# A two-layer streaming trunk in split fp32: the first input block's rows carry the first norm's scales, the second norm's mean squares are summed on all partitions, and the last store is issued by ScalarE's queue

## The chip, the cores and the metric

The kernel runs on one core of one Trainium2 chip. Its time is the device time of one execution in microseconds, given as the median of the runs beside the lowest and highest of them.

## The reference

The input x is 512 frames of 1024 features. One layer (DEPTH is 1) is computed: a first RMSNorm, a wide projection into three branches (A: six heads of forgetting attention, "fox"; B: four heads of a gated linear recurrence in chunks, "hgrn"; C: a causal depthwise convolution of 31 taps over 256 channels), three sigmoid gates that merge the branches, an output projection with a residual, and then a second RMSNorm with a gated feed-forward network and another residual.

```python
def rmsnorm(x, g):
    y = x32 * lax.rsqrt(jnp.mean(x32 * x32, axis=-1, keepdims=True) + EPS)
    return y * g
...
h = rmsnorm(x, norm_mix_g[l])
z = h @ w_in[l]
(fq, fk, fv, ff, hq, hf, hi, hg, ca, cb, gl) = jnp.split(z, IN_SPLITS, axis=-1)
...                                   # ya: attention, yb: recurrence, yc: convolution
gates = jax.nn.sigmoid(gl + gate_b[l])
merged = gates[:, :, 0] * (ya @ wb_a) + gates[:, :, 1] * (yb @ wb_b) + gates[:, :, 2] * (yc @ wb_c)
x = x + merged @ w_out[l]
h2 = rmsnorm(x, norm_ffn_g[l])
gate_in, value_in = jnp.split(h2 @ w_up[l], 2, axis=-1)
x = x + (jax.nn.silu(causal_dwconv(gate_in, ...)) * value_in) @ w_down[l]
```

## The kernel before

Activations are held transposed: features on the 128 partitions, the 512 frames along the row, in eight blocks (`x0` to `x7`). Every fp32 factor is split into a high and a low part (`x0h`, `x0l`; weights `wh_...`, `wl_...`), and each product is three matmuls: high by high, high by low, low by high. A block of 128 output columns over 1024 features is thus a unit of 24 matmuls of 128x512 into one PSUM bank. A weight unit is loaded by one DMA of SyncE's queue (`wr_...`), cast by ScalarE (`wh_...`) and subtracted by VectorE (`wl_...`). The norms are applied late: the products are made from x times the norm's gain, and the result is multiplied by the frame's reciprocal root mean square (`n1rB`, `n2rB`, the same row on all partitions) when VectorE takes it out of PSUM (`evac`).

No engine's order is written by hand. Every operation is recorded in a `Plan` by `record` (so that the profile gives nearly all of them line 110, and tiles tell them apart); `schedule` then plays the program through with a cost for each operation. Each of the five engines takes, of the operations whose inputs are there, the one of the lowest priority number for which a buffer is free, and the order that comes out is what the engines run, each strictly in it. The priority is the place in the program, less a large number for classes such as `FIRST` (loads and splits of the input), `EVAC` (evacuations) and `YOUT`. The counts of buffers are in `CAPS`: 75 full rows of 128x512 (kind "s"), eight PSUM banks (kind "ps") of which at most five hold projections ("mm") and at most six hold everything else ("aux"). An operation that starts a tile is passed over as long as its kinds are used up, and one of a higher number goes ahead.

In the stretch that the prediction speaks of, the third and last unit of the branch-B output gate (`hg`) is followed by the first merge gates: `gate(n)` makes three units `gl` (one for each branch), each evacuated into a row `gr`. Six `gate` calls stand ahead of the first `merge`. Between these units the last pieces of hgrn heads 2 and 3 and the six fox heads are woven in. A head of the recurrence is a chain of small steps: `khT` (transposes of the decayed keys), `pl` (scores within a block, at seven levels), `pst` (state), `pi` (output). VectorE and ScalarE make each step's operands (`d`, `ed`, `ql`, `kl`) and take its result (`at`, `st`, `ob`). A fox head's scores `sp` lie in "aux" banks until VectorE adds the bias and takes the minimum in one instruction (`dd`, with its accumulator row `mn`). The convolution is 60 tap instructions of VectorE (`cv`, two tiles of 30) that run when VectorE has nothing of lower number; their inputs are the rows `xca`.

The first norm's gains are the first eight columns of `pr`, which a DMA of its own brings in. The second norm sums eight squares in `acc2`; `norm_rstd` multiplies its four blocks by a column of ones on TensorE (`n2ms`, frames on the partitions), takes the root there in four columns, and `spread` transposes them (`n2rT`), writes them to memory (`n2dr`) and reads them back on all partitions (`n2rB`).

Of the kernel before, what the change touches and what calls it, by code (L numbers as in the profile page):

```python
# [10 lines left out]
F32 = mybir.dt.float32  # L11
F32R = mybir.dt.float32r
# [7 lines left out]
KT = D // P  # L20
# [27 lines left out]
for _name, _w in (("ident", 128), ("ones", 128), ("onesD", 32)):  # L48
# [1 line left out]
    _n += _w  # L50
NCST = _n
CAPS = {"s": 75, "bm": 2, "tiny": 24, "wraw": 3, "whi": 3, "wlo": 3, "ps": 8, "mm": 5, "aux": 6,
        "d": 2, "ed": 3, "cB": 4, "dd": 3, "pp": 3, "pT": 8}
NCB = NM * (NM + 1) // 2 * P
NLV = 2
NAHEAD = 6
NWARM = 5
FIRST, WPREP, STAT, EVAC, YOUT = -4000000, -3000000, -2000000, -1000000, -1000000


# [4 lines left out]
class Plan:  # L65
# [73 lines left out]
    def schedule(self):  # L139
        ops = self.ops  # L140
        last = {}
        for op in ops:
            op.left = len(op.deps)
            op.ready = 0.0
            for d in op.deps:
                d.users.append(op)
            for n in op.uses:
                last[n] = last.get(n, 0) + 1
        used = {k: 0 for k in self.caps}
        live = set()  # L150
        free = {e: 0.0 for e in ("tensor", "vector", "scalar", "gpsimd", "sync")}
        soon = {e: [] for e in free}
        now_ = {e: [] for e in free}
        releases = []
        for op in ops:
            if not op.left:
                heapq.heappush(soon[op.eng], (op.ready, op.seq, op))
        t, done, order = 0.0, 0, []
        while done < len(ops):
            while releases and releases[0][0] <= t:  # L160
                _, n = heapq.heappop(releases)
                for k in self.kind[n]:
                    used[k] -= 1
            for e in free:
                while soon[e] and soon[e][0][0] <= t:
                    op = heapq.heappop(soon[e])[2]
                    heapq.heappush(now_[e], (op.pri, op.seq, op))
            moved = False
            for e in free:
                if free[e] > t or not now_[e]:  # L170
                    continue
                put = []
                while now_[e]:
                    it = heapq.heappop(now_[e])
                    op = it[2]
                    need = {}
                    for n in op.uses:
                        if n not in live:
                            for k in self.kind[n]:
                                need[k] = need.get(k, 0) + 1  # L180
                    if all(used[k] + c <= self.caps[k] for k, c in need.items()):
                        for n in op.uses:
                            live.add(n)
                            last[n] -= 1
                        for k, c in need.items():
                            used[k] += c
                        op.start = t
                        op.end = t + op.dur
                        free[e] = op.end
                        for n in op.uses:  # L190
                            if not last[n]:
                                heapq.heappush(releases, (op.end + op.lat, n))
                        for u in op.users:
                            hop = 0.0 if (u.eng == e == "tensor") else op.lat
                            u.ready = max(u.ready, op.end + hop)
                            u.left -= 1
                            if not u.left:
                                heapq.heappush(soon[u.eng], (u.ready, u.seq, u))
                        order.append(op)
                        done += 1  # L200
                        moved = True
                        break
                    put.append(it)
                for it in put:
                    heapq.heappush(now_[e], it)
            if moved:
                continue
            nxt = [f for e, f in free.items() if f > t and now_[e]]
            nxt += [s[0][0] for s in soon.values() if s and s[0][0] > t]
            nxt += [max(s[0][0], free[e]) for e, s in soon.items() if s]  # L210
            if releases:
                nxt.append(releases[0][0])
            nxt = [x for x in nxt if x > t]
            if not nxt:
                raise RuntimeError("no instruction can start: " + str(
                    {e: [(o[2].seq, o[2].uses) for o in now_[e][:3]] for e in now_}) + str(used))
            t = min(nxt)
        self.length = max(op.end for op in ops)
        return order
# [57 lines left out]


@with_exitstack
def body(ctx: ExitStack, tc, xT, wct, wt3, wt1, wdn, par, cst, rst, msk, cmk, out):  # L280
    cpool = ctx.enter_context(tc.tile_pool(name="cpool", bufs=1))
    spool = ctx.enter_context(tc.tile_pool(name="spool", bufs=CAPS["s"]))
    wpool = ctx.enter_context(tc.tile_pool(name="wpool", bufs=3))
# [12 lines left out]
    def slot(name, dt=F32, kind=None):  # L296
        return nc.tile(spool, [P, S], dt, "s", nm(name), ("s", kind) if kind else ("s",))
# [78 lines left out]
        nc.vector.scalar_tensor_tensor(lo, src, g, hi.bitcast(F32), op0=ALU.mult, op1=ALU.subtract)  # L376
        return hi, lo

    def evac(ps, name, rb):
        with nc.at(EVAC):  # L380
            t = slot(name)
            nc.vector.tensor_tensor(t, ps, rb, op=ALU.mult)
        return t

    def strided(t, offset, dims):
        return bass.AP(t.tensor, t.offset + offset, [list(t.ap[0]), *map(list, dims)])

    def rsqrt(v, n, name):
        t = tiny(name + "t", n, I32)
        nc.vector.tensor_single_scalar(t, v.bitcast(I32), 1, op=ALU.logical_shift_right)  # L390
        y = tiny(name + "y", n)
        nc.vector.tensor_scalar(y.bitcast(I32), t, -1, 0x5f3759df, op0=ALU.mult, op1=ALU.add)
        for it in range(3):
            a = tiny(name + "a", n)
            nc.vector.scalar_tensor_tensor(a, y, -0.5, y, op0=ALU.mult, op1=ALU.mult)
            nc.vector.tensor_tensor(a, a, v, op=ALU.mult)
            y2 = tiny(name + f"y{it}", n)
            nc.vector.scalar_tensor_tensor(y2, a, 1.5, y, op0=ALU.add, op1=ALU.mult)
            y = y2
        return y  # L400
# [46 lines left out]
    with nc.at(FIRST):  # L447
        nc.table("sigmoid_and_others")
        for _ in range(NWARM):
            nc.tensor.matmul(wps[:, :256], warm[:, :P], warm[:, :256], start=True, stop=True)  # L450
    cuts = ((0, 1), (1, 2), (2, 3), (3, 4), (4, 6), (6, 8))
    xg, w0, sums = [], [], []
    xs = [slot(f"x{kt}") for kt in range(KT)]

    def first_weights():
        k0, k1 = cuts[len(w0)]
        src = wt3[k0 // 2][:, (k0 % 2) * 384:(k0 % 2) * 384 + (k1 - k0) * 384]
        raw = nc.tile(bpool, [P, 2 * S], F32, "bm", nm("wr_hi"), ("bm",)) if len(w0) in (3, 4) else None
        w0.append(wunit(src, (k1 - k0) * 384, f"hi{len(w0)}", FIRST, raw))

    for kt in range(KT):
        with nc.at(FIRST):
            nc.sync.dma_start(xs[kt], xT[:, kt, :])
            if kt == 0:
                nc.sync.dma_start(pr[:, :KT], par[:, :KT])
            if kt == 4:
                nc.sync.dma_start(pr[:, KT:], par[:, KT:])
        if kt in (0, 1, 2, 3, 5):
            first_weights()
        with nc.at(FIRST):  # L470
            xg.append(split_scaled(xs[kt], pc("g1", kt), f"x{kt}"))
        with nc.at(STAT):
            q = slot(f"n1sq{kt}")
            added = nc.scalar.activation(q, xs[kt], AF.Square)
            if kt:
                nc.vector.tensor_tensor(sums[0], sums[0], q, op=ALU.add)
            else:
                sums.append(q)
# [448 lines left out]
    merged, gates, x1, xg2 = [], [], [], []  # L927

    def gate(n):
        gates.append([evac(gemm_c(15 + 3 * n + br, xg, f"gl{n}{br}"), f"gr{n}{br}", rb1) for br in range(3)])  # L930

    def merge(n):
        gts = gates[n]
# [26 lines left out]


    acc2 = None
    for n in range(KT):
        ps = gemm_c(47 + n, merged, f"wo{n}")
        with nc.at(EVAC):
# [6 lines left out]
            else:  # L972
                acc2 = q
    with nc.at(EVAC):
        rt2, rb2 = norm_rstd([acc2], "n2")


    gT = []
# [14 lines left out]
    for n in range(KT):  # L993
# [6 lines left out]
        for c0, c1 in parts:  # L1000
            with nc.at(EVAC):
                nc.vector.tensor_tensor(x1[n][:, c0:c1], ps[:, c0:c1], x1[n][:, c0:c1], op=ALU.add)
            nc.sync.dma_start(out[n][:, c0:c1], x1[n][:, c0:c1])

    nc.issue(tc)

# [1 line left out]
def _layout(i):  # L1008
# [49 lines left out]
    for L in LEVELS:  # L1058
# [4 lines left out]
    c = np.ascontiguousarray  # L1063
    return {
        "xT": c(x.T.reshape(KT, P, S).transpose(1, 0, 2)), "wct": c(wct), "wt3": c(wt3), "wt1": c(wt1),
        "wdn": c(wdn), "par": c(par), "cst": c(cst), "rst": c(rst), "msk": c(msk), "cmk": c(cmk)}


_ORDER = ("xT", "wct", "wt3", "wt1", "wdn", "par", "cst", "rst", "msk", "cmk")


# [14 lines left out]
```

## Time and profile before

| quantity | value |
|---|---|
| median of 3 runs | 804.49 us (804.33 to 804.51) |
| the profiled execution's own time | 804.38 us |
| its span, first to last instruction | 802.5 us |
| TensorE busy | 797.6 us, 99% of the span |
| VectorE, ScalarE, GpSimd busy | 496.4, 336.6, 86.0 us |

The span is what the trace covers; the own time holds 1.9 us more around it. Busy times are of the whole span, so an engine that is half busy in the mean can be nearly full in one stretch. The "chain that ended last" is followed back from the last instruction to whatever released it at each step, and the time that it spends on an engine is the time that a change must shorten to be seen.

### The profile page before, as it was taken

The page shows a single profiled execution, that of the slowest core. Times are in us where ns is not written, and L with a number is a line of the kernel's source. Part 1 is how long each engine was busy: PE and PEld are TensorE (multiplying, and loading weights), DVE is VectorE, ACT ScalarE, POOL GpSimd, SP SyncE. Part 2 cuts the span into 40 slices and gives each one's busy share as a digit, 9 for nine tenths or more (in the row PEclk, how much of TensorE's full clock was granted, in tenths as well). Part 3 has the DMA queues.
Part 4 walks back from the last instruction along what each step waited for, and adds up shares of the span by engine and source line. Part 5 has one row for each costly group of instructions (what it writes and reads, how often), then busy time and mean ns, then how long its engine had stood idle before and what let it go on. Part 6 is the DMA issues. An engine that isn't in the chain of part 4 may idle for free.

```text
span 802.5 us, 10175 instructions
## 1 busy us (share of the span) xinstructions
PE 797.6 (99%) x3911; PEld 677.0 (84%) x3911; DVE 496.4 (62%) x804; ACT 336.6 (42%) x547; POOL 86.0 (11%) x78
## 2 busy tenths in 40 slices
PE   9999999999999999999999999999999999999998
PEld 8889999888888888888888888888888888888886
DVE  6588898988888878556655465555555455222221
ACT  7247556554656328433244254333333333111110
POOL 2000000100122000114422021111101111000000
PEclk9999999999999999999999999999999999999999
DMA  8522132422477222323422322322322332334320
GB/s 306 182 69 83 60 118 79 106 100 79 120 166 181 93 104 80 118 103 133 145 97 87 119 84 100 105 94 91 105 100 85 105 99 82 102 112 128 101 86 26
DMA packets 30880, 86.96 MB, mean 108 GB/s; under 512 B 3640, under 2 KB 7786, under 8 KB 30832
## 3 DMA queue, kind: packets, MB, share of 16 engines
q1 hardware_dynamic: 28240, 82.39, 30.3%
q0 software_dynamic: 2592, 3.93, 3.2%
q8 instruction: 30, 0.49, 0.3%
q14 instruction: 18, 0.15, 0.1%
HBM read 84.17 MB, written 2.14 MB: 108 GB/s over the span
## 4 chain that ended last, share of the span: by engine, by line
PE 99%; DVE 0%; DVEq 0%; issue 0%
PE gl L110 17%; PE ug L110 15%; PE uv L110 15%; PE dn L110 15%; PE br L110 5%; PE wo L110 5%; PE hf L110 3%; PE hq L110 3%; PE pl L110 3%; PE fvm L110 2%; PE him L110 2%; PE f0m L110 2%; PE f1m L110 2%; PE hg L110 2%; PE cb L110 1%; PE ca L110 1%
## 5 line engine op out<-in xcount | busy, mean ns | idle before, releaser
L110 DVE TENSOR_TENSOR wl_wd<-wr_wd,wh_wd 128x1024 fp32r<-128x1024 f32 (+1 forms) x24 | 27.3, 1136 | 65.9 <-ACT wh_wd L110 65.9
L110 ACT CAST wh_wd<-wr_wd 128x1024 fp32r<-128x1024 f32 (+1 forms) x24 | 23.6, 983 | 85.6 <-PE dn L110 81.8
L110 DVE TENSOR_TENSOR wl_ug<-wr_ug,wh_ug 128x1024 fp32r<-128x1024 f32 x22 | 27.0, 1225 | 49.6 <-ACT wh_ug L110 49.6
L110 POOL TENSOR_TENSOR fy<-fy,n2rB 128x512 f32<-128x512 f32 x22 | 28.9, 1317 | 207.8 <-ACT fy L110 207.8
L110 DVE SCALAR_TENSOR_TENSOR cv<-xca,pr,cv 128x511 f32<-128x511 f32 (+29 forms) x60 | 43.5, 729 | 0.3
L110 ACT CAST wh_uv<-wr_uv 128x1024 fp32r<-128x1024 f32 x22 | 23.2, 1054 | 44.4 <-PE ug L110 37.0
L110 ACT CAST wh_gl<-wr_gl 128x1024 fp32r<-128x1024 f32 x24 | 25.3, 1053 | 35.2 <-PE gl L110 21.4
L110 POOL DMA_DIRECT2D cB<-cdr x18 | 16.0, 1093 | 213.7 <-DMA cdr<-cT 122.8
L110 ACT CAST wh_ug<-wr_ug 128x1024 fp32r<-128x1024 f32 x22 | 23.2, 1055 | 31.1 <-PE uv L110 23.6
L110 POOL TENSOR_TENSOR gr<-gr,gr 128x512 f32<-128x512 f32 x14 | 21.6, 1546 | 113.9 <-DVE gr L110 113.2
L110 DVE SCALAR_TENSOR_TENSOR fy<-ug,pr,fy 128x511 f32<-128x511 f32 (+1 forms) x44 | 32.8, 747 | 1.0 <-ACT fy L110 0.3
L110 DVE TENSOR_TENSOR wl_gl<-wr_gl,wh_gl 128x1024 fp32r<-128x1024 f32 x24 | 31.5, 1311 | 2.3 <-ACT wh_gl L110 2.2
L110 DVE TENSOR_TENSOR gr<-gl,n1rB 128x512 f32<-128x512 f32 x24 | 16.6, 692 | 25.3 <-PE gl L110 25.3
L110 DVE TENSOR_TENSOR wl_uv<-wr_uv,wh_uv 128x1024 fp32r<-128x1024 f32 x22 | 27.0, 1225 | 8.5 <-ACT wh_uv L110 8.5
L110 DVE TENSOR_TENSOR ug<-ug,n2rB 128x512 f32<-128x512 f32 x22 | 15.1, 691 | 25.4 <-PE ug L110 25.3
L110 ACT ACTIVATE fy<-fy 128x512 f32<-128x512 f32 x22 | 13.9, 632 | 39.4 <-DVE fy L110 39.4
L110 PEld LDWEIGHTS pl<-ql,kl 128*128 128x128 f32 (+2 forms) x224 | 21.3, 161 | 2.2 <-issue 0.8
L110 DVE TENSOR_TENSOR x<-dn,x 128x512 f32<-128x512 f32 (+1 forms) x9 | 5.6, 631 | 27.3 <-PE dn L110 27.3
L110 PE MATMUL pl<-ql,kl 128*128 128x64 f32 (+2 forms) x224 | 21.3, 242 | 0.0
L110 DVE TENSOR_TENSOR gr<-gr,br 128x512 f32<-128x512 f32 x24 | 16.2, 682 | 5.5 <-PE br L110 5.4
L110 ACT ACTIVATE fy<-ug,pr 128x512 f32<-128x512 f32 x22 | 17.8, 812 | 1.9 <-DVE ug L110 1.9
L110 DVE TENSOR_TENSOR d<-bm 128x520 f32<-128x520 f32 (+5 forms) x24 | 18.1, 773 | 0.0
(1128 smaller groups left out, 2540.2 us busy)
## 6 DMA issues: line engine op xcount, KB each, us to landing
wr_gl<-wct SPq DMA_DIRECT2D x24, 512.0 KB, 3.2
wr_ug<-wct SPq DMA_DIRECT2D x22, 512.0 KB, 3.3
wr_uv<-wct SPq DMA_DIRECT2D x22, 512.0 KB, 3.3
wr_wd<-wdn SPq DMA_DIRECT2D x16, 512.0 KB, 3.5
x<-xT SPq DMA_DIRECT2D x16, 256.0 KB, 4.6
wr_wb<-wct SPq DMA_DIRECT2D x8, 512.0 KB, 3.2
wr_wo<-wct SPq DMA_DIRECT2D x8, 512.0 KB, 3.1
wr_wd<-wdn SPq DMA_DIRECT2D x8, 384.0 KB, 3.1
```

The lines of the kernel that those rows point to most:

```text
L110: op.fn = lambda: fn(*args, **kw)
```

## The change

There are three parts, and two planner rules that go with them. **Start.** The input block `x0` now comes with the eight columns of gains behind its 512 columns, from a new input `x0g`; the separate DMA of the gains is gone, `x0`'s split reads its gain there, and VectorE copies the eight columns into `pr` for the other blocks. `x0` moves from a row of kind "s" to a buffer of kind "bm" (two of 128x1024), one weight unit moves from "bm" to the common weight buffers, and the fifth warm-up matmul is 128 wide instead of 256. **Second norm.** `acc2` is split, and two 128x512 matmuls with a 128x128 matrix of 1/1024 (`onesr`) give the mean square on every partition at once. The root is then taken over 512 columns instead of four, and the transposes, the way through memory and back are gone. **End.** The second half of the last output block is stored from ScalarE's queue, the first still from SyncE's. **Planner.** The rows `gr` have a kind of their own, "gr" (24, as many as there are), and an operation that starts one is taken only while three rows of kind "s" would stay free behind it (`spare`).

```diff
 CAPS = {"s": 75, "bm": 2, "tiny": 24, "wraw": 3, "whi": 3, "wlo": 3, "ps": 8, "mm": 5, "aux": 6,
-        "d": 2, "ed": 3, "cB": 4, "dd": 3, "pp": 3, "pT": 8}
+        "d": 2, "ed": 3, "cB": 4, "gr": 24, "dd": 3, "pp": 3, "pT": 8}
...
-NWARM = 5
+NWARM = 4
...
-                    if all(used[k] + c <= self.caps[k] for k, c in need.items()):
+                    spare = 3 if "gr" in need else 0
+                    if all(used[k] + c + (spare if k == "s" else 0) <= self.caps[k] for k, c in need.items()):
...
+        nc.tensor.matmul(wps[:, :P], warm[:, :P], warm[:, :P], start=True, stop=True)
...
-    xs = [slot(f"x{kt}") for kt in range(KT)]
+    x0 = nc.tile(bpool, [P, 2 * S], F32, "bm", nm("x0"), ("bm",))
+    xs = [x0[:, :S]] + [slot(f"x{kt}") for kt in range(1, KT)]
...
-        raw = ... if len(w0) in (3, 4) else None
+        raw = ... if len(w0) == 3 else None
...
-            nc.sync.dma_start(xs[kt], xT[:, kt, :])
             if kt == 0:
-                nc.sync.dma_start(pr[:, :KT], par[:, :KT])
+                nc.sync.dma_start(x0[:, :S + KT], x0g)
+                nc.vector.tensor_copy(pr[:, :KT], x0[:, S:S + KT])
+            else:
+                nc.sync.dma_start(xs[kt], xT[:, kt, :])
...
-            xg.append(split_scaled(xs[kt], pc("g1", kt), f"x{kt}"))
+            xg.append(split_scaled(xs[kt], pc("g1", kt) if kt else x0[:, S:S + 1], f"x{kt}"))
...
-        gates.append([evac(gemm_c(15 + 3 * n + br, xg, f"gl{n}{br}"), f"gr{n}{br}", rb1) for br in range(3)])
+        gates.append([evac(gemm_c(15 + 3 * n + br, xg, f"gl{n}{br}"), f"gr{n}{br}", rb1, "gr") for br in range(3)])
...
+    onesr = const("onesr", P, F32R)
+    nc.scalar.activation(onesr, ones, AF.Copy, scale=1.0 / D)
...
-        rt2, rb2 = norm_rstd([acc2], "n2")
+        parts = split(acc2, "n2a")
+        ps = bank("n2ms")
+        for u, part in enumerate(parts):
+            nc.tensor.matmul(ps, onesr, part, start=u == 0, stop=u == 1)
+        v = slot("n2v")
+        nc.vector.tensor_scalar(v, ps, EPS, None, op0=ALU.add)
+        rb2 = rsqrt(v, S, "n2r", lambda name, n, dt=F32: slot(name, dt))
...
-            nc.sync.dma_start(out[n][:, c0:c1], x1[n][:, c0:c1])
+            (nc.sync if c1 - c0 == S or c0 == 0 else nc.scalar).dma_start(out[n][:, c0:c1], x1[n][:, c0:c1])
```

The planner makes a new order for the whole program from this. Two places of it are shown. The numbers in the names are buffer numbers: `gl_702`, `gl_707` and `gl_712` are the three units of the first merge gate, `khT_424` belongs to head 2 of the recurrence. In each row the result stands ahead of the arrow, and "waits" names the engines on whose progress the instruction waits. This is TensorE where `hg` ends and the merge gates begin, before the change:

```order
L110 MATMUL hg_688_775<-x7l_128,wh_hg_686_773 128x512
L110 MATMUL hg_688_775<-x7h_127,wl_hg_687_774 128x512
L110 MATMUL gl_702_789<-x0h_94,wh_gl_700_787 128x512 [waits DVE_49,Activation_49]
L110 MATMUL gl_702_789<-x0l_95,wh_gl_700_787 128x512
L110 MATMUL gl_702_789<-x0h_94,wl_gl_701_788 128x512
L110 MATMUL khT_424<-cs,kh_423 128x128 [waits DVE_49]
```

And TensorE at the same `khT_424` after the change:

```order
L110 MATMUL gl_707_794<-x7l_128,wh_gl_705_792 128x512
L110 MATMUL gl_707_794<-x7h_127,wl_gl_706_793 128x512
L110 MATMUL khT_424<-cs,kh_423 128x128 [waits DVE_49]
L110 MATMUL khT_424<-cs,kh_423 128x128 x2
L110 MATMUL pl_430<-ql_138,kl_54_134 65x64 [waits DVE_49]
L110 MATMUL pl_430<-ql_138,kl_54_134 65x64 x3
L110 MATMUL pl_433<-ql_138,kl_55_135 33x32 [waits DVE_49]
L110 MATMUL pl_433<-ql_138,kl_55_135 33x32 x7
L110 MATMUL pa_449<-pr_361_448,cs 128x4 [waits Activation_49]
```

Before, `khT_424` stands behind three matmuls of the first merge-gate unit, of which 21 follow it; after, it stands behind all 24 of that unit and all 24 of the next, and the rows behind it are steps of the recurrence, with no unit among them.

VectorE around `dd_521`, the instruction that takes the first of six fox score tiles out of its "aux" bank, before the change (the rows "ISA" are the bias-and-minimum instruction and its accumulator):

```order
L110 TENSOR_SCALAR nlk_467<-u_463,l1m 128x512
L110 ISA dd_521,mn_523<-sp_522,cB_514 128x128
L110 ISA mn_523 128x1
L110 TENSOR_TENSOR xhg_689_776<-hg_688_775,n1rB_158 128x512
L110 TENSOR_TENSOR bm_466<-bm_466,nlk_467 128x512
L110 SCALAR_TENSOR_TENSOR cv_649_736<-xca_92_172,pr,cv_649_736 128x487
L110 TENSOR_TENSOR wl_gl_711_798<-wr_gl_709_796,wh_gl_710_797 128x1024
```

And after; where the first dots are stand 19 more taps of the same tile `cv_650`:

```order
L110 SCALAR_TENSOR_TENSOR cv_650_737<-xca_102_182,pr,cv_650_737 128x502
L110 TENSOR_TENSOR qe_469<-xq_375_462,eb_468 128x512
L110 TENSOR_TENSOR wl_gl_721_808<-wr_gl_719_806,wh_gl_720_807 128x1024
L110 SCALAR_TENSOR_TENSOR cv_650_737<-xca_102_182,pr,cv_650_737 128x501
...
L110 ISA dd_521,mn_523<-sp_522,cB_514 128x128
L110 ISA mn_523 128x1
L110 ISA dd_526,mn_528<-sp_527,cB_514 128x256
...
L110 TENSOR_TENSOR gr_703_790<-gl_702_789,n1rB_158 128x512
```

`dd_521` stood ahead of the third `xhg` (the evacuation of `hg`) and one row behind `nlk_467`; it now stands 37 rows behind that `xhg`, behind 30 taps and three low parts of weights, of which `wl_gl_716` and `wl_gl_721` use buffers that `gl_702` and `gl_707` must have left. The evacuation `gr_703` of the first merge-gate unit stands 38 rows further on.

## Rows read from the trace of the kernel before

**Rows 1.** The page: busy time, share of the span and instructions of each engine.

```profile
PE 797.6 (99%) x3911; PEld 677.0 (84%) x3911; DVE 496.4 (62%) x804; ACT 336.6 (42%) x547; POOL 86.0 (11%) x78
```

**Rows 2.** Waits of TensorE, whole span: total us, times, longest.

```profile
PE warm L110 <- DVE warm L110: 1.2, 1, 1.2
```

**Rows 3.** Chain that ended last, 160 to 206 us: start, us, what.

```profile
160.54 1.73 PE sp L110 x12
162.27 16.35 PE hg L110 x72
...
179.31 0.33 PE khT L110 x3
...
184.25 0.47 PE pl L110 x8
...
186.14 0.64 PE pl L110 x16
...
188.59 0.84 PE pl L110 x8
...
203.63 1.59 PE pi L110 x14
```

**Rows 4.** Timeline of VectorE, 172 to 191 us: start, us, instruction, idle before.

```profile
177.74 0.28 DVE L110 CUSTOM_DVE_ANT_0 dd<-sp,cB 128x128 f32<-128x128 f32 x1
...
178.66 0.69 DVE L110 TENSOR_TENSOR xhg<-hg,n1rB 128x512 f32<-128x512 f32 x1 [0.63 <-PE hg L110]
179.26 0.68 DVE L110 TENSOR_TENSOR bm<-bm,nlk 128x512 f32<-128x512 f32 x1
179.86 0.72 DVE L110 SCALAR_TENSOR_TENSOR cv<-xca,pr,cv 128x487 f32<-128x487 f32 x1
180.50 1.22 DVE L110 TENSOR_TENSOR wl_gl<-wr_gl,wh_gl 128x1024 fp32r<-128x1024 f32 x1
...
189.54 0.46 DVE L110 COPY_PREDICATED at<-mk,pl 128x256 f32<-128x256 uint8 x1 [0.66 <-PE pl L110]
```

**Rows 5.** Timeline of VectorE, 262 to 312 us: taps with nothing between.

```profile
286.99 2.99 DVE L110 SCALAR_TENSOR_TENSOR cv<-xca,pr,cv 128x486 f32<-128x486 f32 x4
```

**Rows 6.** Timeline of ScalarE, 176 to 207 us.

```profile
179.67 0.48 ACT L110 COPY khT<-khT 128x384 f32<-128x384 f32 x1 [0.19 <-PE khT L110]
...
184.75 0.37 ACT L110 COPY at<-pl 65x256 f32<-65x256 f32 x1 [0.52 <-PE pl L110]
185.50 1.05 ACT L110 CAST wh_gl<-wr_gl 128x1024 fp32r<-128x1024 f32 x1 [0.38 <-PE gl L110]
```

**Rows 7.** Timeline of all engines, 0 to 15 us.

```profile
1.18 0.42 SPq L110 DMA_DIRECT2D pr<-par  x1
...
1.19 4.63 PE L110 MATMUL warm<-warm 128*128 128x256 f32 x10 [1.19 <-DVE warm L110]
...
3.62 0.63 ACT L110 ACTIVATE n1sq<-x 128x512 f32<-128x512 f32 x1 [1.60 <-DMA x<-xT]
...
4.16 0.71 ACT L110 ACTIVATE x0h<-x,pr 128x512 fp32r<-128x512 f32 x1
...
5.31 1.02 PE L110 MATMUL him<-wh_hi,x0h 128*128 128x384 f32 x3
...
6.17 0.68 PE L110 MATMUL him<-wh_hi,x0l 128*128 128x384 f32 x3
```

**Rows 8.** Busy time by stretch; after the engines the granted clock, DMA share, GB/s.

```profile
798.90:800.90 2.00, 0.00 (x0) 0.00 (x0) 0.74 (x2) 0.00 (x0) 0.00 (x0) 1.00 0.29 101
801.10:802.40 1.30, 0.00 (x0) 0.00 (x0) 0.00 (x0) 0.00 (x0) 0.00 (x0) 0.50 0.01 3
```

**Rows 9.** Chain that ended last, 436 to 470 us.

```profile
443.25 0.81 PE n2ms L110 x8
...
450.76 0.11 PE n2rT L110
```

**Rows 10.** Timeline of VectorE, 438 to 462 us.

```profile
440.80 0.74 DVE L110 SCALAR_TENSOR_TENSOR x27l<-x,pr,x27h 128x512 fp32r<-128x512 f32 x1
...
458.17 1.28 DVE L110 TENSOR_TENSOR ug<-ug,n2rB 128x512 f32<-128x512 f32 x2
```

**Rows 11.** Timeline of all engines, 797 to 803 us.

```profile
798.89 0.76 DVE L110 TENSOR_TENSOR x<-dn,x 128x256 f32<-128x256 f32 x2 [13.36 <-PE dn L110]
799.34 0.82 SPq L110 DMA_DIRECT2D out<-x  x2
```

More of the change, by code (lines that the diff above doesn't have):

```diff
@@ L279, in body @@
 @with_exitstack
-def body(ctx: ExitStack, tc, xT, wct, wt3, wt1, wdn, par, cst, rst, msk, cmk, out):
+def body(ctx: ExitStack, tc, xT, wct, wt3, wt1, wdn, par, cst, rst, msk, cmk, x0g, out):
     cpool = ctx.enter_context(tc.tile_pool(name="cpool", bufs=1))
@@ L377, in split_scaled, with evac @@
         return hi, lo
-    def evac(ps, name, rb):
+    def evac(ps, name, rb, kind=None):
         with nc.at(EVAC):
-            t = slot(name)
+            t = slot(name, kind=kind)
             nc.vector.tensor_tensor(t, ps, rb, op=ALU.mult)
@@ L386, in strided, with rsqrt @@
         return bass.AP(t.tensor, t.offset + offset, [list(t.ap[0]), *map(list, dims)])
-    def rsqrt(v, n, name):
+    def rsqrt(v, n, name, tiny=tiny):
         t = tiny(name + "t", n, I32)
@@ L457, in first_weights @@
         src = wt3[k0 // 2][:, (k0 % 2) * 384:(k0 % 2) * 384 + (k1 - k0) * 384]
-        raw = nc.tile(bpool, [P, 2 * S], F32, "bm", nm("wr_hi"), ("bm",)) if len(w0) in (3, 4) else None
+        raw = nc.tile(bpool, [P, 2 * S], F32, "bm", nm("wr_hi"), ("bm",)) if len(w0) == 3 else None
         w0.append(wunit(src, (k1 - k0) * 384, f"hi{len(w0)}", FIRST, raw))
@@ L1065, in _layout @@
         "xT": c(x.T.reshape(KT, P, S).transpose(1, 0, 2)), "wct": c(wct), "wt3": c(wt3), "wt1": c(wt1),
-        "wdn": c(wdn), "par": c(par), "cst": c(cst), "rst": c(rst), "msk": c(msk), "cmk": c(cmk)}
-_ORDER = ("xT", "wct", "wt3", "wt1", "wdn", "par", "cst", "rst", "msk", "cmk")
+        "wdn": c(wdn), "par": c(par), "cst": c(cst), "rst": c(rst), "msk": c(msk), "cmk": c(cmk),
+        "x0g": c(np.concatenate([x.T[:P], par[:, :KT]], 1))}
+_ORDER = ("xT", "wct", "wt3", "wt1", "wdn", "par", "cst", "rst", "msk", "cmk", "x0g")
 def kernel(**inputs):
```

## The prediction, made before the changed kernel had run

> **What bounds the kernel now.** I began with the page's engine times: TensorE is busy for 797.6 of 802.5 us [rows 1]. TensorE's list of waits has one entry, 1.2 us before its first instruction [rows 2], so between start and end it never stands still. Two things follow. Whatever the change takes off another engine gains nothing unless TensorE is handed less work or begins or ends earlier. And any stop of TensorE that a new order brings goes into the time one to one. So I read the new order for places where TensorE's next instruction waits for something that another engine now does late. There is one such place, at the end of `hg`, and it outweighs the three parts.
>
> **The stop at 190 us.** Before `hg` the chain shows twelve score matmuls, which fill six tiles `sp` [rows 3]: all the "aux" banks. `khT` needs an "aux" bank, so it waits for `dd_521`, the first to empty one. Before the change VectorE did that at 177.74, ahead of the third `xhg` [rows 4], and `khT` ran at 179.31 without a wait [rows 3]. After it, `dd_521` stands behind 30 taps. The planner put them there, I think, because `dd` must open a row of kind "s", while a tap that updates its tile in place opens nothing. The evacuations `gr` stand later still, so only `gl_702` and `gl_707` lie ahead of `khT` on TensorE, and the third unit `gl_712` behind a stretch of the recurrence.
>
> When does TensorE run out? `hg` ends at 162.27 + 16.35 = 178.62, and its 72 matmuls give 16.35 / 3 = 5.45 us a unit [rows 3]. The two units end at 184.07 and 189.52.
>
> When does VectorE reach `dd_521`? From `xhg` at 178.66 to `bm` and from `bm` to the next it takes 0.60 us each, a tap that alternates with taps on the other tile 0.64 (179.86 to 180.50), a low part of weights 1.22 [rows 4]. So: `xhg`, `bm`, `wl`, a small product of about 0.1, and six taps end at 178.66 + 1.20 + 1.22 + 0.1 + 3.84 = 185.0. The next low part needs a cast that waits for the end of `gl_702`: 184.07 + 1.05 [rows 6] = 185.1, and ends at 186.3; four taps and a 512-wide product of 0.6 end at 189.5. The last low part waits likewise for `gl_707`: 189.52 + 1.05 + 1.22 = 191.8. Then 20 taps stand on one tile, each reading what the one before wrote: four such took 2.99 us, against 0.72 for one, so the pitch is (2.99 - 0.72) / 3 = 0.757 [rows 4, 5]. That is 19 x 0.757 + 0.72 = 15.1, to 206.9. `dd` and its accumulator take 0.3 more [rows 4]: `khT` starts at 207.2. **TensorE stands for 207.2 - 189.5 = 17.7 us.**
>
> **What follows the stop.** Up to `gl_712` TensorE has only the recurrence's steps and a few score products. Its own work there, from [rows 3]: two `khT` 0.66, two `pl` of the first kind 0.94, two of the second 1.28, five of 128x64 at 0.84 4.2, one `pi` 1.59, two `pst` at 6/14 of a `pi` 1.4, and eleven others about 1.6: 11.7 us. Before, units of `gl` lay between these and covered every reply; now each step waits for its reply. A 128x64 level is 0.84 of TensorE, 0.46 of the masking copy [rows 4], and a decayed operand of 0.4 to 0.5 that partly overlaps: I take 1.7, so 8.5 for five. The front (copies of 0.37 and 0.48 [rows 6], operands of the like) I put at 3.4, `pst` and `pi` with their copies at 2.2, the rest at 2.3: 16.4. So 16.4 - 11.7 = **4.7 us** idle. If VectorE's 40 rows alone set the pace (about 14.4 us) it is 2.7; at 2.2 us a level it is 7.2. In the unit after it VectorE is again about as loaded as TensorE, for which I add **0.7**, between 0 and 2.
>
> **The clock.** After the last matmul the granted clock stood at 1.00 (2.4 GHz) for two more microseconds and was 0.50 (1.2 GHz) from 801.1 on [rows 8]. A stop of 17.7 us is longer, so TensorE comes out of it at half. How long for, the start bounds: busy from 1.19, its first three products of 128x384 at 5.31 took 1.02, so (1.02 - 0.33) / 2 = 0.345 each with 0.33 the length of one, and those at 6.17 took 0.68, 0.175 each [rows 7]. So about 5.0 us of unbroken work went by at half speed, and the same here would cost 2.5. But this stretch is broken by waits; at half throughout, it costs its whole 11.7. If the clock were back at once it costs 0. I take **5.0**, nearer to the row of the start.
>
> The Trainium skill, page "TensorE: Matmul & The Clock Gate", section "What's actually happening", says that the throttled state is the default and that recent activity lifts it. The rows at the start and at the end agree. By that rule a stretch of short steps with waits between could stay throttled, which is the third case below.
>
> **The three parts.** *Start.* The gains' DMA held SyncE's queue for 0.42 us, and `x0h` stood on ScalarE behind `n1sq` (3.62 against 4.16) [rows 7]; both go. The first products, whose weights' cast and split stand behind `x0h`, can begin some 0.5 earlier, and the warm-up ends 0.43 earlier (one of its ten records of 4.63 / 10 [rows 7]). The five more that wait on later input move up too, if the input was late by its issue. I take **-0.7**, between 0 and -1.1; work at half clock, which every start has, may eat part of it. *Second norm.* The eight `n2ms` of 0.81 and `n2rT` of 0.11 leave TensorE [rows 9], and two 128x512 matmuls of 5.45 / 24 = 0.23 come: **-0.5**. On VectorE eleven steps of four columns become steps of 512, each like the 0.6 to 0.74 of 512-wide rows [rows 4, 10], some 8.6 us with the split. What hides them: five "mm" banks take units while no evacuation runs, so TensorE works on for 5 x 5.45 = 27 us from the first `ug`. Before, the first evacuation came at 458.17 [rows 10]; after, the root is done by about 443.3 + 0.5 + 8.6 + two low parts at 1.22 = 455. If that cover were gone, each microsecond would count in full. *End.* The last two additions start at 798.89, and SyncE issues two stores in 0.82 [rows 11]. Issued side by side, the second can start up to 0.4 earlier, but it waits for the second addition anyway (0.76 for both). The nearest far bound is GpSimd's issue of about 1.1, so -0.1 to +0.7; I take **0**, as ScalarE's queue resembles SyncE's more than GpSimd's.
>
> The Trainium skill, page "Trainium Kernel Development and Optimization", section "Key Constraints", says that transfers issued from several engines share the same DMA engines, and that several queues save only issue time. By it this part is worth at most the issue of one store, half of the 0.82 of that row, and no more in bandwidth.
>
> **The sum.** The profiled execution's own time is 804.38, 0.11 under the median of 804.49, so both serve. 804.38 + 17.7 + 4.7 + 0.7 + 5.0 - 0.7 - 0.5 + 0 = 831.3: **831 us**.
>
> **The rivals.**
> (1) *The stop, and the clock back at once.* The start, where full speed came only after 5.0 us of work [rows 7], speaks against it; for it only that the clock stayed up for two microseconds after the last matmul [rows 8], so it falls late and may rise early. 831.3 - 5.0 = 826.3, and with the serial stretch at its low bound 824; 821 to 827 with what VectorE may save before the stop.
> (2) *The stop, and the clock low until `gl_712`.* The waits between the steps speak for it, the 5.0 us of the start against: 831.3 + 6.7 = 838, up to 843.
> (3) *A smaller stop.* If VectorE passes the casts sooner, or the taps on one tile run at the alternating pitch of 0.64 (2.3 us less), or half of the stop is made up because TensorE's work left in the other units runs without waits: 806 to 821. Against it: TensorE has no later slack to make anything up [rows 2].
> (4) *No stop; the other side.* `khT`'s bank would have to be another than the one `dd_521` frees, one free by 189.5. It decides at this point: VectorE must reach what `khT` waits for within the 10.9 us of `gl_702` and `gl_707`, not 28.5. Then only the parts are left: 804.38 - 0.7 - 0.5 = 803.2. Against it: `khT` waits for VectorE in both orders, and the six tiles fill all "aux" banks.
> (5) *The start's gain does not come*, since TensorE's first products wait for weights and not for gains: 832.0. This lies in the range of the forecast.
>
> **How the numbers follow.** The forecast, with the clock low for a part of the serial stretch (827 to 836, and rival 5 in it), has 0.55; rival 1 0.20; rival 2 0.15; rival 3 0.06; rival 4 0.04. The range from 821 to 840 holds the first two and most of rival 2, about 0.85 in all. A change of 0.2%, 1.6 us, is about what a measurement of this kernel can tell from none. Only rival 4 ends below 806, and at 803.2 it lies on the edge between the two: half of it, 0.02, for faster by more than that, 0.03 within it (the other half and the low edge of rival 3), 0.95 for slower.
>
> **What would show it.** In the changed profile TensorE's waits must have a new entry of 16 to 19 us, `khT` behind VectorE's `dd`, at about 190 us; VectorE must show about 15 us of taps on one tile just ahead of it, with the first `gr` some 14 us or more behind. Between 207 and 224 TensorE must be busy for only about two thirds of the time; the `pl` pieces there tell the clock, 0.84 at full speed and about twice that at half. The first product must start near 4.8, no `n2rT` may be left, and the last matmul must be followed by about 3.6 us as before. I would be wrong if `khT` found a bank early, if VectorE's taps were spread again, or if a second long wait stood at the second norm.

## The result: 837.65 us, 4.2% slower, and the profile after

The changed kernel takes 837.65 us in the median of 4 runs (836.17 to 840.52), against 804.45 of the kernel before beside it; the ratio is 1.0418, with a 95% interval from 1.0404 to 1.0432. The profiled execution took 837.57, with a span of 835.8 us, 33.3 longer than before.

TensorE's list of waits, which had one entry before [rows 2], is the first thing to read (columns: total us, times, longest):

```profile
PE khT L110 <- DVE mn L110: 17.7, 1, 17.7
PE n1rT L110 <- DVE nry L110: 2.2, 1, 2.2
PE pl L110 <- DVE at L110: 1.4, 2, 0.9
PE warm L110 <- DVE warm L110: 1.2, 1, 1.2
PE pst L110 <- DVE rl L110: 0.8, 1, 0.8
PE pl L110 <- DVE mn L110: 0.5, 1, 0.5
PE him L110 <- DVE wl_hi L110: 0.2, 1, 0.2
```

The largest entry is the stop that was forecast at 17.7 us: `khT` behind `mn`, the accumulator row of `dd`. The second, 2.2 us before `n1rT`, was not forecast. Where the first one comes from stands in the chain that ended last; its columns are start, us, what:

```profile
182.00 10.67 PE gl L110 x47
192.74 1.05 ACT wh_gl L110
193.81 1.22 DVE wl_gl L110
...
210.26 0.29 DVE dd L110
210.62 0.92 PE khT L110 x3
...
223.52 1.98 PE pl L110 x8
...
230.75 2.99 PE pi L110 x14
...
236.54 1.85 PE gl L110 x8
```

The chain runs through `gl`, leaves TensorE at 192.67 for the cast and the low part of a weight unit, then goes through 20 taps of VectorE and `dd` to `khT` at 210.62. Before, it did not leave TensorE in this stretch [rows 3]. From `khT` to the third unit of `gl` at 236.54 it takes 25.9 us. Its pieces are slow: a `pl` of eight records takes 1.98 against 0.84 [rows 3], `pi` 2.99 against 1.59. VectorE's timeline shows the taps in one block (start, us, instruction):

```profile
184.46 3.95 DVE L110 SCALAR_TENSOR_TENSOR cv<-xca,pr,cv 128x486 f32<-128x486 f32 x6
...
194.95 15.27 DVE L110 SCALAR_TENSOR_TENSOR cv<-xca,pr,cv 128x501 f32<-128x501 f32 x20
...
235.36 1.28 DVE L110 TENSOR_TENSOR gr<-gl,n1rB 128x512 f32<-128x512 f32 x2
```

Twenty taps on one tile took 15.27 us, a pitch (from the start of one to the start of the next) of (15.27 - 0.73) / 19 = 0.765; six that alternate between two tiles took 3.95, a pitch of about 0.65. The first evacuations `gr` come at 235.36, just ahead of the third unit. The stretches show the clock (busy us and instructions of TensorE, its weight loads, VectorE, ScalarE and GpSimd; then granted clock, DMA share, GB/s):

```profile
33.00:35.60 2.60, 2.60 (x7) 2.00 (x7) 0.00 (x0) 0.04 (x1) 0.00 (x0) 0.50 0.25 91
...
196.00:200.00 4.00, 0.00 (x0) 0.00 (x0) 3.82 (x6) 0.00 (x0) 0.00 (x0) 0.53 0.36 131
...
212.00:216.00 4.00, 3.84 (x32) 3.58 (x32) 3.15 (x7) 2.06 (x6) 0.48 (x1) 0.50 0.37 95
...
228.00:232.00 4.00, 3.19 (x15) 3.00 (x15) 2.68 (x9) 1.02 (x4) 0.86 (x1) 0.50 0.19 52
236.00:240.00 4.00, 4.00 (x23) 3.29 (x21) 4.00 (x12) 3.87 (x14) 0.86 (x1) 1.00 0.26 43
```

TensorE is idle from 196 to 200, comes back at a granted clock of 0.50 (1.2 GHz), and is still at it from 228 to 232, 20 us later. The first row stands behind the other wait, which ended at 31.06 us: the clock was 0.50 from 33 to 35.6.

The rows of the start (all engines):

```profile
1.18 0.42 SPq L110 DMA_DIRECT2D wr_hi<-wt  x1
...
1.19 4.11 PE L110 MATMUL warm<-warm 128*128 128x256 f32 x10 [1.19 <-DVE warm L110]
...
3.58 0.72 ACT L110 ACTIVATE x0h<-x 128x512 fp32r<-128x512 f32 x1 [1.56 <-DMA x<-x0g]
3.58 2.35 DVE L110 COPY pr<-x 128x8 f32<-128x8 f32 x1 [2.44 <-DMA x<-x0g]
...
5.05 0.77 PE L110 MATMUL him<-wh_hi,x0h 128*128 128x384 f32 x3
```

The warm-up is 0.52 shorter, SyncE's second issue is already a weight unit, `x0h` begins at 3.58 instead of 4.16, and the first product at 5.05 instead of 5.31 [rows 7], though not near the 4.8 that was named as a sign. One row was not forecast: VectorE's copy of the eight columns lasts 2.35 us in the trace, to 5.93, the low parts `x0l` and `wl_hi` behind it end at that same time, and TensorE waits 0.2 us for `wl_hi`. What holds VectorE there is not shown. 26 us later VectorE's and TensorE's rows around the first norm's root are these:

```profile
29.71 1.22 DVE L110 TENSOR_TENSOR wl_ca<-wr_ca,wh_ca 128x1024 fp32r<-128x1024 f32 x1 [1.46 <-ACT wh_ca L110]
30.85 0.15 DVE L110 SCALAR_TENSOR_TENSOR nry<-nra,nry 128x4 f32<-128x4 f32 x1
...
31.06 0.27 PE L110 MATMUL n1rT<-cs,nry 128*4 128x128 f32 x1 [2.24 <-DVE nry L110]
```

The last step of the root (`nry`) stands on VectorE behind `wl_ca`, whose cast waits for the end of the first `cb` unit; TensorE, behind `cb`, has nothing but `n1rT`, which needs that step.

At the second norm I compare the first `ug` of the chain, before:

```profile
438.72 4.53 PE ug L110 x20
```

and after, with the two matmuls of the mean square among the units:

```profile
472.55 5.44 PE ug L110 x24
477.99 0.23 PE n2ms L110
...
478.89 0.23 PE n2ms L110
```

The last rows (VectorE, then the two queues) answer to [rows 11]:

```profile
832.08 0.75 DVE L110 TENSOR_TENSOR x<-dn,x 128x256 f32<-128x256 f32 x2 [13.36 <-PE dn L110]
832.53 0.34 SPq L110 DMA_DIRECT2D out<-x  x1
832.86 0.37 ACTq L110 DMA_DIRECT2D out<-x  x1
```

**Where the 33.3 us are.** The end of `hg` moved from 178.62 to 182.00: +3.38, which holds the start's gain and the wait of `n1rT`. The stop is 17.74. From the end of `hg` to the first `ug` it is 33.83 - 3.38 = 30.45 more than before, so the stretch behind the stop costs 30.45 - 17.74 = 12.7; it ends with the third unit, since from 236.54 to 472.55 TensorE is busy throughout at a granted clock of 1.00. From the first `ug` to the last additions it is 33.19 - 33.83 = -0.64. The tail behind them is 3.72 instead of 3.61: +0.1. The sum is 33.3.

### The profile page after: what moved, and what is told of

It is laid out like the page before. It is cut to its first block, busy times and chain, and to the rows that moved or that the text cites. A ratio compares the mean times of both kernels' runs of the same rounds, so it can differ in the third digit from the quotient of the medians.

```text
span 835.8 us, 10144 instructions
## 1 busy us (share of the span) xinstructions
PE 807.7 (97%) x3904; PEld 686.4 (82%) x3904; DVE 507.4 (61%) x805; ACT 336.6 (40%) x549; POOL 86.7 (10%) x78
## 4 chain that ended last, share of the span: by engine, by line
PE 96%; DVE 3%; ACT 0%; DMA 0%; issue 0%; DVEq 0%; ACTq 0%
PE gl L110 16%; PE dn L110 14%; PE uv L110 14%; PE ug L110 14%; PE wo L110 5%; PE br L110 5%; PE pl L110 3%; PE hf L110 3%; PE hq L110 3%; PE fvm L110 2%; PE f0m L110 2%; PE f1m L110 2%; PE him L110 2%; PE hg L110 2%; DVE cv L110 2%; PE ca L110 1%
## 5 line engine op out<-in xcount | busy, mean ns | idle before, releaser
L110 POOL TENSOR_TENSOR fy<-fy,n2ry 128x512 f32<-128x512 f32 x22 | 29.0, 1317 | 207.1 <-ACT fy L110 185.2
L110 DVE TENSOR_TENSOR ug<-ug,n2ry 128x512 f32<-128x512 f32 x22 | 15.1, 690 | 24.9 <-PE ug L110 24.8
L110 PEld LDWEIGHTS pl<-ql,kl 128*128 128x128 f32 (+2 forms) x224 | 24.9, 189 | 3.3 <-DVE mn L110 0.9
L110 PE MATMUL pl<-ql,kl 128*128 128x64 f32 (+2 forms) x224 | 25.7, 272 | 1.2 <-DVE mn L110 0.5
L110 PE MATMUL khT<-cs,kh 128*128 128x128 f32 x12 | 3.4, 351 | 17.7 <-DVE mn L110 17.7
```

Of the source, the lines that this page charges most:

```text
L110: op.fn = lambda: fn(*args, **kw)
```

## The experiments

Three of the 75 rows are set apart for `dd`, so that it needs no free row of kind "s":

```diff
-CAPS = {"s": 75, ...
+CAPS = {"s": 72, ...
...
-                dd = slot("dd", kind="dd")
+                dd = nc.tile(ddpool, [P, S], F32, "dd", nm("dd"), ("dd",))
```

> The changed kernel, with three of the 75 rows of kind s set apart for the fox rows dd (72 are left for all else). Theory A (dd stood behind the 30 taps only because it had to open a row of kind s and none was free; all that followed, the serial stretch and the low clock in it, comes from that one wait): the 17.7 us wait of khT goes, the low clock between 192 and 233 us goes, the 2.2 us wait of n1rT stays with the low clock after it; 805.5 to 808.5 us. Rival B (the rule that keeps three rows free for the gates, or the rows moved at the start, starve the recurrence by themselves): khT or gl waits again by more than 5 us, 815 us or more.

Measured: 805.59 us, 1.0018 times the kernel before (1.0009 to 1.0026). All three parts and the planner's rules are in it, and 32 of the 33 us are gone. Of TensorE's waits one is left beside the first:

```profile
PE n1rT L110 <- DVE nry L110: 2.2, 1, 2.2
```

Theory A holds and B falls: what put `dd` behind the taps was the want of a row. The planner of the changed kernel, played through with its own costs, says the same: whenever the turn of `dd` comes, all 75 rows are in use, until the last of the 20 taps has ended; the row that comes free then, and that `dd` takes, is `xca`, which that tap is the last to read. So the taps did not merely stand ahead of `dd`; they had to end before it could start. The wait of `n1rT` is there as expected, but this time without a low clock behind it (the stretch from 33 to 35.6 in this run):

```profile
33.00:35.60 2.60, 2.60 (x13) 2.17 (x12) 0.00 (x0) 0.23 (x1) 0.00 (x0) 1.00 0.32 123
```

The second experiment leaves the count of rows alone and only holds the taps back until the first `dd` has run:

```diff
-    conv()
+    with nc.after(*dds[:1]):
+        conv()
```

> The changed kernel, with the convolution's taps held back until the first dd has run. Theory A (VectorE's order, dd behind the taps, is the cause): no wait of khT, no low clock near 200 us; 806 to 812 us, since the taps now come later and may crowd the last gates. Rival B (the rows themselves are missing, whoever runs first): dd is still late and khT waits by more than 5 us, 815 us or more.

Measured: 807.27 us (1.0039, 1.0025 to 1.0052), with no wait of `khT`; `n1rT` waits 2.2 us, a unit of `gl` 1.0 us for a cast, and `him` 0.5 us. The stop goes again, as theory A has it, but this edit does not part the theories: taps that are held back do not open their two rows `cv` either (`dd` runs at 179.99 here, the first instruction of `cv` at 192.75), so `dd` also finds a row. Both of these runs repair the stop by changes that touch nothing of the three parts, and in both `dd` has a row in time.

The third takes only the second norm and the last store into the kernel before; the edit is those hunks of the change's diff.

> The kernel before, with only the second norm on all partitions and the last store from ScalarE's queue; start and planner rules as before. Theory A (these two parts are harmless, and the norm saves what leaves TensorE): 0.4 to 0.8 us under the kernel before, 803.7 to 804.1. Rival C (the root over 512 columns is late for the first evacuations, or the second queue is late): 805 or more, with a wait of TensorE at 460 to 470 us or a longer tail than 3.65 us after the last matmul.

Measured: 803.53 us against 804.18, ratio 0.9989 (0.998 to 0.9998), and no wait but the first. The 512-wide root is covered, and these two parts together gain 0.65 us.

The fourth asks what the stop does beyond its own length. The bank of the second unit gets 78 more products by zeros, so that TensorE works where it stood:

```diff
+        if zeros is not None:
+            for k in range(78):
+                nc.tensor.matmul(ps, zeros, acts[n - 1][0], start=False, stop=k == 77)
```

> The changed kernel, with 78 more matmuls of 128x512 by a matrix of zeros at the end of the second merge-gate unit, so that TensorE is busy for 17.7 us where it stood. The result is unchanged; the order of all else is too. Theory D (the idle stop lowers the clock, and the low clock makes the recurrence's steps behind it slower): the granted clock is 1.00 all through, the stretch from khT to the third unit falls from 25.8 us to 16 to 20, and the time to 828 to 832 us. Rival E (the replies of VectorE and ScalarE set the pace of that stretch, not TensorE's clock): the stretch stays within 2 us of 25.8 and the time at 836 to 838.

Measured: 834.72 us (1.0387, 1.0368 to 1.0406). The chain's rows (start, us, what) and the stretches:

```profile
208.81 0.56 PE khT L110 x3
...
217.68 1.99 PE pl L110 x8
...
230.29 1.85 PE gl L110 x8
```

```profile
192.00:209.00 17.00, 16.92 (x76) 13.71 (x75) 16.04 (x23) 0.00 (x0) 0.00 (x0) 1.00 0.10 32
...
212.00:216.00 4.00, 3.59 (x28) 3.10 (x28) 3.43 (x8) 2.70 (x8) 1.71 (x2) 1.00 0.56 133
216.00:220.00 4.00, 3.09 (x16) 2.71 (x16) 2.26 (x6) 2.37 (x8) 0.00 (x0) 0.61 0.52 78
220.00:224.00 4.00, 2.62 (x11) 2.46 (x12) 2.88 (x10) 2.08 (x8) 0.00 (x0) 0.50 0.16 49
```

Neither theory holds as it was put. The stretch from `khT` to the third unit fell from 25.9 to 230.29 - 208.81 = 21.5 us, short of the 16 to 20 of theory D and beyond the 2 us of theory E. With TensorE busy up to `khT`, the clock stayed at 1.00 until about 216, and then fell to 0.50 all the same, in a stretch in which TensorE was busy for 3.6 and then 3.1 of 4 us; the `pl` at 217.68 took 1.99 again. So the idle stop is not the only thing that the clock falls behind: it fell here within the broken stretch, with no long stop before it. Of the 5 us that this profiled run (832.61) gained, 1.8 came ahead of the stop, most of it where its clock did not fall behind the wait of `n1rT`; the stretch gave 4.4, and 1.3 were lost again behind the third unit.

The next one repairs both waits, with `spare` at 0 and the low parts of the `ca` units held back by the root:

```diff
+        roots.append(nc.ops[-1])
...
+            with nc.after(*behind):
+                nc.vector.tensor_tensor(lo[:, :n], raw[:, :n], hi[:, :n].bitcast(F32), op=ALU.subtract)
...
-        xca = evac(gemm_c(12 + 2 * j, xg, f"ca{j}"), f"xca{j}", rb1)
+        xca = evac(gemm_c(12 + 2 * j, xg, f"ca{j}", roots), f"xca{j}", rb1)
```

> The three parts of the change (start, second norm, store) with three rows set apart for dd, without the rule that keeps three rows free for the gates, and with the low parts of the two ca weight units held behind the last step of the first norm's root. Theory A (the whole loss is two waits made by the order: khT behind dd, n1rT behind the root; the parts themselves gain 0.7 at the start and 0.6 at the norm): no wait of TensorE but the first, 802.4 to 803.3 us, 0.9 to 1.8 under the kernel before. Rival F (the start's 0.7 is lost again in the stretch behind it, whatever the order): 803.4 to 804, as with the norm and the store alone.

Measured: 804.46 us, 0.9999 (0.999 to 1.0008): no gain, and above the ranges of both theories. `n1rT` no longer waits, but the new order has another wait, which theory A had not allowed for:

```profile
PE po L110 <- DVE pl L110: 1.3, 1, 1.3
```

By the end of `hg` this profile is 0.73 us ahead of the kernel before, at the first `ug` 0.45 behind it, and the stretch from there gains 0.64 again. So the parts' gain was there and was lost between `hg` and `ug`, where that wait stands. Whether it is lost whatever the order, as rival F has it, the last two runs ask.

The planner's rule alone, in the kernel before, tells whether that rule makes the stop. (The start's part alone can't be asked: without the rule, or rows for `dd`, the planner comes to a state in which no instruction can start.)

> The kernel before, with only the rule that an evacuation of a gate unit leaves three rows of kind s free. Theory A (the rule alone does not put dd behind the taps; the start's rows and the rule together do): no wait of khT of 17 us; a few waits of 1 to 2 us among the recurrence's steps, 804.5 to 810 us. Rival G (the rule alone makes the stop): khT waits by 15 us or more, 825 us or more.

Measured: 811.30 us (1.0081, 1.0052 to 1.011), a little above the range, and no wait of `khT`. Rival G falls: the rule alone does not make the stop. The stop was seen only with the start's rows and the rule together. The rule has a price of its own, and little of it is idle time: TensorE's new waits sum to 2.4 us. The rest is in the stretches of this run:

```profile
192.00:196.00 4.00, 3.67 (x25) 3.10 (x24) 3.37 (x7) 3.02 (x7) 0.00 (x0) 1.00 0.00 0
196.00:200.00 4.00, 2.16 (x15) 1.91 (x15) 3.95 (x12) 1.92 (x7) 0.00 (x0) 0.88 0.39 131
200.00:204.00 4.00, 4.00 (x24) 4.00 (x23) 3.11 (x8) 2.10 (x8) 0.86 (x1) 0.50 0.42 119
208.00:212.00 4.00, 4.00 (x19) 3.90 (x19) 2.79 (x8) 2.00 (x5) 0.43 (x1) 0.50 0.39 65
```

A stretch in which TensorE was busy for 3.7 and then 2.2 of 4 us, with waits of at most about 1 us each, was followed by some 14 us at a granted clock of 0.50. For 11 of them, from 200 to 211 us, the trace shows TensorE at short steps without any wait, and the clock stayed down.

The start's part with rows for `dd`, and nothing else, asks where the wait of `n1rT` comes from:

> The kernel before, with the start's part alone and three rows set apart for dd (without them the start's part finds no order at all). Theory H (the wait of n1rT comes from the start, whose earlier casts let a low part of a ca unit go ahead of the root's last step): n1rT waits 2 to 2.5 us, the time is 0.5 to 0.8 above the kernel with all three parts and three rows for dd, 806.0 to 807.0 us. Rival I (that wait comes from the second norm or the free-rows rule): no wait of n1rT, 803.3 to 804.0.

```profile
PE n1rT L110 <- DVE nry L110: 2.2, 1, 2.2
PE po L110 <- DVE pl L110: 1.6, 1, 1.6
```

Measured: 808.23 us (1.0051, 1.0038 to 1.0063). The wait of 2.2 us is there with the start's part alone, so theory H is right on its origin; the time is 1.2 above its range. This order has the wait of `po` too, 1.6 us that the range did not hold, and the granted clock between 24 and 36 us was 0.86.

The last two ask whether the parts can be had. In the first the low parts of the attention weights go ahead of weight units, on top of both repairs:

```diff
+                with nc.at(FIRST):
+                    nc.vector.tensor_tensor(lo[:, :w], ptp[:, :w], hi[:, :w].bitcast(F32), op=ALU.subtract)
```

> As the kernel with everything repaired, but the low parts of the attention weights (pl, taken from ptp) go ahead of weight units on VectorE, where 1.3 us of TensorE's waiting was left (po behind pl). Theory A (each microsecond that TensorE stands counts in full, and the parts gain 0.7 and 0.6): that wait goes, 802.8 to 803.4 us, 1.0 to 1.6 under the kernel before. Rival F (a new wait comes in its place, as it did with the last repair): 804 or more.

Measured: 803.03 us against 804.36, ratio 0.9983 (0.9974 to 0.9992), with no wait but the first one. It beats both kernels, by 1.33 us against the one before, as theory A has it. Its profile is 0.37 us ahead by the end of `hg`, 0.33 more by the first `ug`, and 0.64 more by the last additions: the norm's gain in full, the start's in part, and a third piece that no row explains.

> As the kernel before it in this list, but only the second ca unit's low part is held behind the root, and gates leave one row free: another order of the whole program out of the same parts. Theory A: 802.6 to 803.8 us if no wait of TensorE over 0.3 us is left, and above that by the sum of those that are. Rival F: 804 or more without such a wait.

Measured: 805.78 us (1.0018, 1.0008 to 1.0028), and its runs lie between 803.2 and 807.6. Again one new wait, in the profiled run of 804.78:

```profile
PE cvt L110 <- DVE mn L110: 1.4, 1, 1.4
```

With that 1.4 subtracted, this profile is within theory A's range, but the median of the runs is 1.0 above the profiled one and outside it, and no profile shows why. So the gain can be had in one order, and another order of the same parts loses it.

## Why the prediction was right, and where its terms were off

**The main step held to a tenth.** The wait of `khT` was forecast at 17.7 us and measured at 17.74. Its parts were right too: 20 taps in 15.1 against 15.27, `dd` and `khT` behind the last low part. TensorE ran out of work at 192.88 instead of 189.5 and `dd` began at 210.26 instead of 206.9, both 3.4 later, as the end of `hg` was. The first experiment, with the second beside it, shows that the row that `dd` wants, and so its place behind the taps, is the cause; rivals 3 and 4 are out.

**"There is one such place" was wrong.** The sentence on what bounds the kernel looked for late answers, and found one of two. The start's own term, -0.7, was right, so rival 5 is out too: the last piece of `him` in the chain (start, us, what) ends at 8.62 + 14.52 = 23.14 before,

```profile
8.62 14.52 PE him L110 x82
```

and 0.74 earlier, at 22.40, after; the second row is the first `ca` unit behind the wait:

```profile
6.01 16.39 PE him L110 x93
...
31.33 7.08 PE ca L110 x24
```

Yet at the end of `hg` the sum stood at +3.38. Between them lie the wait of `n1rT`, 2.24, and that `ca` unit, which took 7.08 us at the low clock and 5.46 in the first experiment, where the clock was 1.00; some 0.3 is in smaller pieces. VectorE's last root step had slipped behind a low part, which waits for a cast, which waits for TensorE. The start's part brings it (seventh run; neither the second norm and the store alone nor the rule alone has it). I had priced the instructions that the start's part removes and not the order behind it. That missing term is 4.1 us, the largest single error; about 1.6 of it is the low clock behind the wait, which some runs have and some don't.

**The stretch behind the stop was under-sized.** Forecast were 4.7 and 0.7 of idle time and 5.0 for the clock, 10.4 together; measured were 12.7. The split was off by more. The five 128x64 levels alone took about 5 x (1.98 - 0.84) = 5.7 more at the low clock, and with `pi`, `pst`, `khT` and the first `pl` the clock cost about 10; TensorE's waits there sum to 2.7. At half speed TensorE itself covers most of the replies: from 210.62 to 236.54 it was busy for 22.95 of 25.92 us, not for the two thirds that were named as a sign. This is rival 2's mechanism, the clock low for nearly the whole stretch until `gl_712`. The step that failed is "nearer to the row of the start": that row was unbroken work, and this stretch was not. The row was also a weak ground: its 5.0 us at half speed were read from the length of the products, while the granted clock of the kernel before, in the profile's stretch over the start, is 1.00:

```profile
1.20:5.60 4.40, 4.40 (x11) 3.47 (x11) 0.70 (x2) 2.46 (x4) 4.20 (x10) 1.00 0.75 229
```

Why those products took twice as long at that reading stays open. The filled stop shows that the clock can fall in the broken stretch where no long stop stands ahead of it. How much of the 21.5 us that it then took is replies and how much is clock stays open.

The clock rule of the Trainium skill, page "TensorE: Matmul & The Clock Gate", section "What's actually happening" (throttled by default, lifted by recent activity), agrees with these rows only in part: 0.50 from 210.62 to about 233.7 us, in short steps with waits between them, and 1.00 from 234 on; but from 216 to 220 us the trace shows TensorE busy throughout, and the clock stayed at 0.50.

**The second norm and the store** were right: -0.64 against -0.5, +0.1 against 0. The first evacuation with the new root came 19.5 us after the first `ug` (492.08 less 472.55), just as before (458.17 [rows 10] less 438.72), so the longer chain of VectorE cost TensorE no wait.

The sum by these measures is 804.4 + 3.4 + 17.7 + 12.7 - 0.6 + 0.1 = 837.7. The forecast of 831 was low by 6.4 in the parts: 4.1 at the first norm, 2.3 behind the stop, and nothing at the stop. The measured 837.65 lies above the 827 to 836 of the forecast's own case; the range holds it only because it reaches into rival 2. Rival 2's 838 is nearly met, but that is luck: its stretch was to cost 4.7 + 0.7 + 11.7 = 17.1 us and cost 12.7, and the 4.1 at the first norm, which no case had, made up for it.

## What to carry to other kernels

Where a planner decides the order, a small edit is not small: moving one buffer and guarding three rows cost 33 us, and the same three parts, with three rows set apart and without the guard, gained 1.3 in another order. Before counting what an edit removes, go through the new order for each instruction of the bounding engine that waits, and ask on its releaser's engine what now stands ahead of it, including what that in turn waits for. A buffer that is wanted by a short instruction on the critical chain is best not drawn from a pool that everything else fills: here the row came free only when 20 instructions of bulk work had ended.

## What was not expected of the hardware

The granted clock of TensorE fell without a long stop. In the run with the filled stop it went from 1.00 to 0.50 at about 217 us, and in the run with the planner's rule alone between 196 and 200 us, in both cases in the midst of short steps with waits of about 1 us or less between them. In the second of these runs it then stayed at 0.50 from 200 to 211 us, in short steps without a wait; so the absence of waits did not bring it back there. A single wait of 2.24 us, the same instruction at the same place, was followed by a low clock in the changed kernel (0.50 from 33 to 35.6 us) and not in the first experiment (1.00), which makes 7.08 - 5.46 = 1.6 us of difference between runs of nearly the same program. What decides between the two is not shown.
